# Output-weight sums by accumulating DMAs, and a lighter branch B, in a hybrid attention layer

## The chip, the cores and the metric

One core of one Trainium2 chip runs the whole layer in one launch. The metric is the device time of one execution in microseconds (us), the median of several runs. The engines are TensorE (PE), VectorE (DVE), ScalarE (ACT), GpSimd (POOL) and SyncE (SP), which here only issues DMAs.

## What is computed

One layer on 528 positions (512 and 16 learned meta tokens), width 2048. The stream is normalised and projected once (`u @ w_in`) into the columns of two attention branches, their gates and two merge gates.

- Branch A picks 128 keys for each query by an indexer score and attends to latent keys, 8 heads of 128.
- Branch B takes, for each of 8 heads, `softmax(q1 k1 + bias) - lambda * softmax(q2 k2 + bias)` over chunk-causal keys (64 wide), times the values, and then a root-mean-square norm of every head's output, times a weight:

```python
attn = probs(q1, k1) - lam * probs(q2, k2)
...
o_b = (rms_norm(o_b, subln_w) * (1.0 - lam_init)).reshape(Bsz, T, B_WIDTH)
y_a = (o_a * jax.nn.silu(z_a)) @ w_o_a
y_b = (o_b * jax.nn.silu(z_b)) @ w_o_b
mix = jax.nn.sigmoid(g_a) * y_a + jax.nn.sigmoid(g_b) * y_b
out = mix @ w_out
return h + rms_norm(out, post_w)
```

## The kernel before, in words

The work is laid out in stages, each bound to its matmuls: the first weights and the norm (0 to 78 us), the indexer's projections (to 183), branch B (to 536), branch A (to 775), the gates with a Strassen-like scheme on 2x2 halves (`Pair`, `Run`; to 1221), the two output projections `wo` with the merge (to 1396), and the last product with `w_out`, again in a Strassen-like scheme.

**Weights.** Every weight block is loaded as float32 (`raw`, L144 in the indexer's stage, L179 for a `Unit`, both on SP's queue), squared on ACT with a sum by rows (L117), its maximum taken over the partitions on POOL (`over_rows`, `rows`, L122), turned into a power of two by tiny operations on DVE (`power_of_two`, L129 to L135), and split into a high and a low half-precision part (ACT L161, DVE L162), which PE multiplies (L265 to L267). So PE can't start on a unit before POOL has given its `rows`.

**Branch B.** For head `h` the loop (L845 to L866) projects q, k and v and, between those projections, takes a step of head `h-1`, kept in `pending`: `vprep`, four query blocks `blk(0..3)`, `tr` (PE transposes the probabilities `pr`, L658) and `pv`. Rounds of branch A's top-k (`run_topk`, MAX8 and MATCH_REPLACE8 on DVE) stand between too. `blk` makes two logits, `softmax` for each (DVE adds the bias and takes the maximum, L643; L647 or L649 negates it; ACT takes the exponent, L651), normalises both with the reciprocals of their sums (L724 to L726) and joins them (L727). `kstack` splits the keys of both halves, each copied to both halves of the partitions (ACT `kh` L752 and L753, DVE `kl` L755).

**Sums of output weights.** The last product needs four differences of quarters of `w_out`, for 16 pieces (k, n). `wt_load` (L251) loads four tiles 128x512 on SP's queue, `wt_sums` (L258) takes four differences on DVE (L261) and writes them with four DMAs of ACT's queue to `wout_t1` to `wout_t4`. Heads 1 to 7 of branch B do two pieces each, the `wo` stage the last two. `tc.keep_in_program_order` keeps those loads where they are written.

**GpSimd.** POOL also adds the bias to branch A's scores (L817), takes half of the differences of `t_prep` (L877, L879), multiplies branch B's outputs with their norm (`load_o`, L1048), and clears a corner of the bias tile (L636).

**What sets the order.** The kernel is written for a framework that reorders: a list scheduler gives each engine and queue one fixed order, by its own estimates, and puts in the waits. An instruction that waits holds up all that stands behind it on its engine, DMAs that this engine issues included. Loads stay in a few buffers; at most eight DMAs of a kind (hardware queue, or POOL's) are under way before the ninth waits for the first.

```python
def wt_sums():
    k, n, (b11, b12, b21, b22) = wt["loaded"].pop(0)
    for i, (o, x, y) in ((0, (b11, b12, b11)), (2, (b12, b22, b12)), (1, (b22, b22, b11)), (3, (b21, b21, b22))):
        nc.vector.tensor_sub(o, x, y)
        nc.scalar.dma_start(tscr[i][k, :, 512 * n:512 * n + 512], o)
```

Of the kernel before, what the change touches and what calls it, by code (L numbers as in the profile page):

```python
# [68 lines left out]
def layer_kernel(ctx, tc, xt_d, xn_d, cols_d, w0_d, wi_d, wkv_d, wo_d, wout_d, lam_d, post_d,  # L69
# [11 lines left out]
    msq = nc.dram_tensor("o_sumsq", [NH, 512], F32, kind="Internal").ap()  # L81
    rsq = nc.dram_tensor("o_rstd", [NH, 512], F32, kind="Internal").ap()
# [36 lines left out]
    def over_rows(ssq):  # L119

        r = wpool.tile([P, 16], F32, tag="rows", name="rows", bufs=4)[:, :ssq.shape[1]]
        nc.gpsimd.partition_all_reduce(r, ssq, P, bass_isa.ReduceOp.max)  # L122
        return r

    def power_of_two(r, exps):
# [8 lines left out]
        nc.vector.tensor_scalar(sc[:, 0:1], t, -1.0, SFIELD * EXP1, op0=ALU.mult, op1=ALU.add)  # L134
        nc.vector.tensor_scalar(sc[:, 1:2], t, exps, None, op0=ALU.add)  # L135
# [3 lines left out]
    def exps_with(dst, un, less=0.0):  # L139
        nc.vector.tensor_scalar(dst, un.bitcast(I32), (UFIELD - 127.0 - less) * EXP1, None, op0=ALU.add)  # L140
# [30 lines left out]
    class Unit:  # L171
# [14 lines left out]
        def scale(self):  # L186
            self.s, self.un = power_of_two(self.rows, uexp[:, 1:2] if self.key[0] == "qb" else uexp[:, 0:1])
            self.hi = wpool.tile([P, KT, P], F16, tag="hi", name="hi", bufs=2)
            self.lo = wpool.tile([P, KT, P], F16, tag="lo", name="lo", bufs=2)
# [56 lines left out]
    wt = {"next": 0, "loaded": []}  # L246

    def wt_load(pool, tags):
        k, n = divmod(wt["next"], 2)
        wt["next"] += 1  # L250
        t = []  # L251
        for tag, (ci, di) in zip(tags, ((0, 0), (0, 1), (1, 0), (1, 1))):
            t.append(pool.tile(HB, F32, tag=tag, name="wt"))
            d = nc.sync.dma_start(t[-1], wout_d[ci, di, k, :, 512 * n:512 * n + 512])
            tc.keep_in_program_order(d)
        wt["loaded"].append((k, n, t))

    def wt_sums():  # L258
        k, n, (b11, b12, b21, b22) = wt["loaded"].pop(0)
        for i, (o, x, y) in ((0, (b11, b12, b11)), (2, (b12, b22, b12)), (1, (b22, b22, b11)), (3, (b21, b21, b22))):  # L260
            nc.vector.tensor_sub(o, x, y)  # L261
            nc.scalar.dma_start(tscr[i][k, :, 512 * n:512 * n + 512], o)
# [200 lines left out]
    def u_scale():  # L463
# [4 lines left out]
        s, un = power_of_two(over_rows(gsum), UFIELD * EXP1)  # L468
        nc.vector.tensor_scalar(gs, cols[:, :KT], s, None, op0=ALU.mult)
        exps_with(uexp[:, 0:1], un)  # L470
        exps_with(uexp[:, 1:2], un, 3.0)
# [147 lines left out]

    PH = ap_.tile([P, 11, P], F32R, name="PH")  # L620
# [12 lines left out]
    def bias_tile(h):  # L633
        g = ap_.tile([P, T], F32, tag="G", name="G", bufs=2)
        nc.sync.dma_start(g, bass.AP(tensor=frep, offset=h * P * NF + P - 1, ap=[[NF - 1, P], [1, T]]))
        nc.gpsimd.memset(g[:64, T - 64:T], NEG)  # L636
        return g

    def softmax(srcs, bias, dst, mx, z):
        at = 0  # L640
        for i, x in enumerate(srcs):
            n = x.shape[1]
            nc.vector.tensor_tensor_reduce(dst[:, at:at + n], x, bias[:, at:at + n], 1.0, -3.0e38,  # L643
                                           ALU.add, ALU.max, mx[:, i:i + 1])
            at += n
        if len(srcs) == 2:
            nc.vector.tensor_scalar(mx[:, :1], mx[:, :1], mx[:, 1:2], -1.0, op0=ALU.max, op1=ALU.mult)  # L647
        else:
            nc.vector.tensor_scalar(mx[:, :1], mx[:, :1], -1.0, None, op0=ALU.mult)  # L649
        mx = mx[:, :1]  # L650
        nc.scalar.activation(dst, dst, AF.Exp, bias=mx, accum_out=z)  # L651
# [39 lines left out]
    def b_attend(h, q, kk, vt):  # L691
        q1, q2 = q
# [17 lines left out]
        def blk(b):  # L710
            mx = ap_.tile([P, 8], F32, tag="mx", name="mx", bufs=MXB)
            z = ap_.tile([P, 2], F32, tag="z", name="z", bufs=3)
            n = NKB[b]
            gb = g[:, T - n:T]
            dst = [pr[b], ap_.tile([P, T], F32, tag="p2", name="p2", bufs=4)[:, :n]]
            for m, qm in ((0, q1), (1, q2)):
                qs = qm[:, b * P:(b + 1) * P]
                src = []
                for s in [slice(0, NLB[b])] if b < 3 else [slice(0, TH), slice(TH, T)]:
                    lg = bank1()  # L720
                    mm2(lg[:, :s.stop - s.start], qs, kk[m][0][:, s], kk[m][1][:, s])
                    src.append(lg[:, :n if b < 3 else TH])
                softmax(src, gb, dst[m], mx[:, 2 * m:2 * m + 2], z[:, m:m + 1])
# [21 lines left out]

    def kstack(acc, un):
        out = [[ap_.tile([P, T], F32R, tag="kk", name=n, bufs=6) for n in ("kh", "kl")] for _ in range(2)]
        for t in range(2):
            s = slice(TH * t, TH * t + TH)
            for m, (kh, kl) in enumerate(out):  # L750
                hs, os_ = slice(64 * m, 64 * m + 64), slice(64 - 64 * m, 128 - 64 * m)
                nc.scalar.activation(kh[hs, s], acc[t][hs, :TH], AF.Copy, scale=un[hs])  # L752
                nc.scalar.activation(kh[os_, s], acc[t][hs, :TH], AF.Copy, scale=un[hs])  # L753
                for d in (hs, os_):
                    nc.vector.scalar_tensor_tensor(kl[d, s], acc[t][hs, :TH], un[hs], f32(kh[hs, s]),  # L755
# [488 lines left out]
    for c in range(KT):  # L1244
# [20 lines left out]
        if c in (4, 7):  # L1265
            wt_sums()
# [188 lines left out]
```

## Time and profile before

| | |
|---|---|
| median of 3 runs | 1559.57 us (1557.87 to 1562.82) |
| the profiled execution | 1558.4 us, of which the span of the trace is 1556.6 us |
| PE busy | 1443.3 us, 93% of the span |
| DVE, ACT, POOL busy | 1161.6, 982.9, 150.3 us |
| mean granted clock of PE | 0.971 |
| DMA | 246.7 MB, mean 158 GB/s |

PE is the engine to read against: what the kernel can win is PE's idle time and the time in which PE runs at the lower of its two clocks (1.2 instead of 2.4 GHz, shown as 0.50). The time beside the span (1.8 us) is start and end and stays as it is.

### The profile page before, as it was taken

What the parts mean: (1) busy time and instruction counts of PE and PEld (TensorE: products, weight loads), DVE (VectorE), ACT (ScalarE), POOL (GpSimd) and SP (SyncE); (2) the same over time, 40 slices, a digit from 0 to 9 for tenths busy, and PEclk for the clock granted to TensorE, in tenths of its full rate; (3) what the DMA queues carried; (4) which work ended last, traced back from release to release, by engine and by line L of the source; (5) the groups of instructions that cost most, each with busy time, mean ns of one, the idle gap of its engine ahead of it and who ended that gap; (6) DMA issues with size and microseconds to landing.
All of it is one profiled execution on the core that took longest, in us unless ns stands there. A gap on an engine that the chain in (4) does not pass through costs nothing. (4 is left out here: it accounts for less than half of the span.)

```text
span 1556.6 us, 25582 instructions
## 1 busy us (share of the span) xinstructions
PE 1443.3 (93%) x9474; PEld 1079.9 (69%) x9474; DVE 1161.6 (75%) x2328; ACT 982.9 (63%) x1749; POOL 150.3 (10%) x203
## 2 busy tenths in 40 slices
PE   7899998898988898999998889999999899999997
PEld 7688766766666666556587768888888544458885
DVE  7975888778888786565677777787778566566778
ACT  7364676656566676666676677777778544436555
POOL 3500000000000022212001100000000011000001
PEclk9899999999999999999999989999999999999999
DMA  6482365445545433122544534444445566446774
GB/s 208 147 272 77 123 203 163 151 141 190 196 140 193 136 116 118 53 96 69 186 155 154 162 116 136 137 141 135 135 144 166 186 211 205 147 167 225 240 248 147
DMA packets 98141, 246.70 MB, mean 158 GB/s; under 512 B 11144, under 2 KB 15432, under 8 KB 97888
## 3 DMA queue, kind: packets, MB, share of 16 engines
q1 hardware_dynamic: 81424, 215.44, 43.5%
q10 hardware_dynamic: 16592, 29.64, 5.1%
q8 instruction: 74, 1.21, 0.3%
q14 instruction: 51, 0.42, 0.1%
HBM read 203.01 MB, written 47.39 MB: 161 GB/s over the span
## 5 line engine op out<-in xcount | busy, mean ns | idle before, releaser
L969 PEld LDWEIGHTS <-wh 128*128 128x128 f16 x2464 | 243.5, 99 | 66.7 <-issue 25.0
L117 ACT ACTIVATE junk<-raw 128x1024 bf16<-128x1024 f32 x192 | 202.1, 1053 | 116.7 <-DMA raw<-in_wi_dram 84.9
L265 PE MATMUL acc<-u,hi 128*128 128x264 f16 (+1 forms) x832 | 267.6, 322 | 1.0 <-DVE kal L783 1.0
L266 PE MATMUL acc<-u,hi 128*128 128x264 f16 (+1 forms) x832 | 267.0, 321 | 0.0
L267 PE MATMUL acc<-u,lo 128*128 128x264 f16 (+1 forms) x832 | 267.0, 321 | 0.0
L969 PE MATMUL acc<-tu,wh 128*128 128x256 f16 x1408 | 237.3, 275 | 20.9 <-DVE r L978 16.1
L969 PE MATMUL acc<-tu,wl 128*128 128x256 f16 x704 | 193.5, 275 | 0.0
L969 PE MATMUL acc<-u,wh 128*128 128x256 f16 x1056 | 180.2, 277 | 9.9 <-ACT wh L161 9.9
L161 ACT ACTIVATE hi<-raw,scale 128x1024 f16<-128x1024 f32 x104 | 118.0, 1143 | 108.2 <-PE acc L266 106.2
L162 DVE SCALAR_TENSOR_TENSOR lo<-raw,scale,hi 128x1024 f16<-128x1024 f32 x104 | 132.9, 1283 | 41.9 <-ACT hi L161 41.2
L265 PEld LDWEIGHTS <-hi 128*128 128x128 f16 x1088 | 108.2, 99 | 79.8 <-issue 6.6
L267 PEld LDWEIGHTS <-lo 128*128 128x128 f16 x1088 | 108.0, 99 | 76.8 <-issue 1.9
L162 DVE SCALAR_TENSOR_TENSOR wl<-S,scale,wh 128x1024 f16<-128x1024 f32 x88 | 115.3, 1311 | 59.8 <-ACT wh L161 59.6
L266 PEld LDWEIGHTS <-hi 128*128 128x128 f16 x1088 | 108.1, 99 | 74.3 <-issue 2.1
L969 PE MATMUL acc<-u,wl 128*128 128x256 f16 x528 | 146.3, 277 | 3.5 <-DVE wl L162 3.5
L122 POOL PARTITION_ALL_REDUCE rows<-ssq x90 | 47.8, 531 | 974.9 <-ACT junk L117 880.6
L969 PEld LDWEIGHTS <-wl 128*128 128x128 f16 x1232 | 121.9, 99 | 20.1 <-DVE wl L162 4.8
L161 ACT ACTIVATE wh<-S,scale 128x1024 f16<-128x1024 f32 x88 | 100.2, 1140 | 33.5 <-DVE S L1076 33.5
L267 PE MATMUL acc<-og,lo 128*128 128x512 f16 x256 | 97.0, 379 | 0.0
L265 PE MATMUL acc<-og,hi 128*128 128x512 f16 x256 | 97.0, 379 | 0.0
L266 PE MATMUL acc<-og,hi 128*128 128x512 f16 x256 | 97.0, 379 | 0.0
L162 DVE SCALAR_TENSOR_TENSOR wl<-raw,scale,wh 128x1024 f16<-128x1024 f32 x66 | 85.4, 1294 | 14.1 <-ACT wh L161 14.0
(309 smaller groups left out, 2978.1 us busy)
## 6 DMA issues: line engine op xcount, KB each, us to landing
raw<-in_wi_dram SPq DMA_DIRECT2D x172, 512.0 KB, 4.3
wt<-in_wout_dram SPq DMA_DIRECT2D x64, 256.0 KB, 4.6
wout_t<-wt ACTq DMA_DIRECT2D x64, 256.0 KB, 3.1
raw<-in_wo_dram SPq DMA_DIRECT2D x32, 512.0 KB, 3.9
raw<-wout_t SPq DMA_DIRECT2D x32, 512.0 KB, 3.9
raw<-in_wout_dram SPq DMA_DIRECT2D x24, 512.0 KB, 4.8
sg<-r ACTq DMA_DIRECT2D x32, 256.0 KB, 3.3
sg<-sg SPq DMA_DIRECT2D x32, 256.0 KB, 3.0
```

The lines of the kernel that those rows point to most:

```text
L117: nc.scalar.activation(j, src, AF.Square, accum_out=dst)
L122: nc.gpsimd.partition_all_reduce(r, ssq, P, bass_isa.ReduceOp.max)
L161: nc.scalar.activation(hi, src, AF.Copy, scale=s)
L162: nc.vector.scalar_tensor_tensor(lo, src, s, hi, op0=ALU.mult, op1=ALU.subtract)
L265: nc.tensor.matmul(out, aH, bH, start=start, stop=False)
L266: nc.tensor.matmul(out, aH, bL, start=False, stop=False)
L267: nc.tensor.matmul(out, aL, bH, start=False, stop=stop)
L969: nc.tensor.matmul(acc, a[:, k, :], b, start=first and k == 0 and x == 0, stop=last and x == 2, skip_group_check=True)
```

## The change

Four things change.

1. **Branch B.** The first softmax is left unnormalised: its sum goes into `Z1`, the joined row is `p1 - lambda*z1/z2 * p2`, and the norm of the head's output takes care of the factor, with `eps * z1^2` in its root; `put_sums` writes the sums once. The maximum is taken negated in the same DVE operation, the exponent with scale -1. The low parts of the keys are made once, not for both halves (`kl`, one tile), the copies of the high parts come by two small DMAs on ACT's queue, and ACT writes two more tiles `QZ` of the queries (zeros in the other half).
2. **Powers of two.** Two tiny DVE operations become one.
3. **Output-weight sums.** `wt_chain` replaces `wt_load` and `wt_sums`: two loads on SP, then DMAs of POOL's queue that add another quarter from DRAM into the tile, and puts, now on SP's queue, between them. In all 32 loads, 64 accumulating DMAs and 64 puts instead of 64 loads, 64 subtractions on DVE and 64 puts on ACT's queue. The signs move to `mix_sums` and to one multiplication of `post` by -1. The loads are no longer kept in program order.
4. **GpSimd.** L817, L877, L879, L1048 and the corner of L636 move to DVE.

The diff, cut to its core:

```diff
-        nc.vector.tensor_scalar(sc[:, 0:1], t, -1.0, SFIELD * EXP1, op0=ALU.mult, op1=ALU.add)
-        nc.vector.tensor_scalar(sc[:, 1:2], t, exps, None, op0=ALU.add)
+        nc.vector.scalar_tensor_tensor(sc, sgn, t, ex, op0=ALU.mult, op1=ALU.add)
...
+    def wt_chain(k, n, tags):
+        t = [opool.tile(HB, F32, tag=tag, name="wt") for tag in tags]
+        q = [[wout_d[ci, di, k, :, 512 * n:512 * n + 512] for di in range(2)] for ci in range(2)]
+        def put(i, x):
+            nc.sync.dma_start(tscr[i][k, :, 512 * n:512 * n + 512], x)
+        def add(x, src):
+            nc.gpsimd.dma_start(x, src, accum_op=ALU.add)
+        nc.sync.dma_start(t[0], q[0][0])
+        nc.sync.dma_start(t[1], q[0][1])
+        yield
+        add(t[0], q[0][1])
+        add(t[1], q[1][1])
+        yield
+        put(0, t[0])
+        put(2, t[1])
+        yield
+        add(t[1], q[0][0])
+        yield
+        put(1, t[1])
+        yield
+        add(t[1], q[1][0])
+        yield
+        put(3, t[1])
...
-            nc.vector.tensor_tensor_reduce(dst[:, at:at + n], x, bias[:, at:at + n], 1.0, -3.0e38,
-                                           ALU.add, ALU.max, mx[:, i:i + 1])
+            nc.vector.tensor_tensor_reduce(dst[:, at:at + n], x, bias[:, at:at + n], -1.0,
+                                           mx[:, i - 1:i] if i else 3.0e38, ALU.add, ALU.min, mx[:, i:i + 1])
...
-            nc.vector.reciprocal(z, z)
-            nc.vector.tensor_mul(z, z, pscale)
-            nc.vector.tensor_scalar(dst[0], dst[0], z[:, 0:1], None, op0=ALU.mult)
+            nc.vector.reciprocal(z[:, 1:2], z[:, 0:1])
+            nc.vector.tensor_scalar(z[:, 1:2], z[:, 1:2], zs, nlam, op0=ALU.mult, op1=ALU.mult)
             nc.vector.scalar_tensor_tensor(dst[0], dst[1], z[:, 1:2], dst[0], op0=ALU.mult, op1=ALU.add)
...
+    def qstack(acc, un, h):
+        q = stack64(acc, un, ap_, "q", 4)
+        for m in range(2):
+            hs = slice(64 * m, 64 * m + 64)
+            nc.scalar.activation(QZ[h % 2][m][hs], acc[hs], AF.Copy, scale=un[hs])
+        return list(q) + QZ[h % 2]
...
+            for m in range(2):
+                hs = slice(64 * m, 64 * m + 64)
+                nc.scalar.activation(kh[m][hs, s], acc[t][hs, :TH], AF.Copy, scale=un[hs])
+                nc.vector.scalar_tensor_tensor(kl[hs, s], acc[t][hs, :TH], un[hs], f32(kh[m][hs, s]),
+                                               op0=ALU.mult, op1=ALU.subtract)
+        for m in range(2):
+            hs, os_ = slice(64 * m, 64 * m + 64), slice(64 - 64 * m, 128 - 64 * m)
+            nc.scalar.dma_start(f32(kh[m][os_]), f32(kh[m][hs]))
...
-            nc.gpsimd.tensor_add(gm[:, :n], g[:, T - n:T], SC[b])
+            nc.vector.tensor_add(gm[:, :n], g[:, T - n:T], SC[b])
...
     for h in range(NH):
+        for i in range(2):
+            wt_now.append(wt_chain(h, i, [f"o{6 + 4 * (h % 2) + 2 * i + x}" for x in range(2)]))
...
-            nc.gpsimd.tensor_mul(o, o, r)
+            nc.vector.tensor_mul(o, o, r)
```

**The order that the change makes.** SP's queue at the end of the indexer's stage, before (`raw_1466` is the 11th of twelve weight halves of that stage, `raw_1570` the 12th, the others belong to the first units):

```order
L144 DMA raw_1466<-in_wi_dram 128x1024 [waits DMAHW3_49,DMAHW1_49,DVE_49]
L179 DMA raw_1527<-in_wi_dram 128x1024 [waits DMAHW6_49,DMAHW2_49,DVE_49]
L179 DMA raw_1529<-in_wi_dram 128x1024 [waits DMAHW7_49,DVE_49]
L179 DMA raw_1538<-in_wi_dram 128x1024 [waits DMAHW4_49,DMAHW0_49,DVE_49]
```

The same place after the change (`raw_1467` is the 11th half, `raw_1528` the first unit's; DMASW is the semaphore of a DMA that POOL issued):

```order
L152 DMA raw_1467<-in_wi_dram 128x1024 [waits DMAHW0_49,DVE_49]
L260 DMA wout_t2<-wt_2324 128x512 [waits DMAHW1_49,DMASW4_49]
L265 DMA wt_2856<-in_wout_dram 128x512 [waits DMAHW2_49]
L260 DMA wout_t2<-wt_2328 128x512 [waits DMAHW3_49,DMASW6_49]
L260 DMA wout_t1<-wt_2851 128x512 [waits DMAHW4_49,DMASW5_49]
L260 DMA wout_t3<-wt_2852 128x512 [waits DMAHW5_49,DMASW7_49]
L260 DMA wout_t1<-wt_2855 128x512 [waits DMAHW6_49,DMASW0_49]
L187 DMA raw_1528<-in_wi_dram 128x1024 [waits DMAHW7_49,DVE_49]
```

The scheduler has moved the chains of all sixteen pieces into the indexer's stage and the first units of branch B: a unit's load now stands behind puts, each of which waits until an accumulating DMA has landed.

POOL from the indexer's stage into branch B, before (`rows` of the units; the memsets prepare branch B):

```order
L122 ISA rows<-ssq 128x2 x2
L625 MEMSET PH 128x128
L625 MEMSET PL 128x128
L625 MEMSET MS 80x512
```

and after, where 27 accumulating DMAs stand ahead of these rows:

```order
L128 ISA rows<-ssq 128x2
L263 DMA wt<-in_wout_dram 128x512 x8
L128 ISA rows<-ssq 128x2
L263 DMA wt<-in_wout_dram 128x512 x18
L646 MEMSET PH 128x128
```

Fifty-four of the 64 additions are issued before the third `rows`, the last two just before the eighth.

DVE around the joining of `pr_3338`, the last block of a head of branch B, before (`kl` and `lo` belong to the next head's keys and weights, MAX to the top-k):

```order
L755 SCALAR_TENSOR_TENSOR kl<-acc,scale,kh 64x264 x2
L724 RECIPROCAL z<-z 128x2
L755 SCALAR_TENSOR_TENSOR kl<-acc,scale,kh 64x264
L725 TENSOR_TENSOR z<-z,pscale 128x2
L755 SCALAR_TENSOR_TENSOR kl<-acc,scale,kh 64x264
L726 TENSOR_SCALAR pr_3338<-pr_3338,z 128x528
L162 SCALAR_TENSOR_TENSOR lo<-raw,scale,hi 128x1024
L727 SCALAR_TENSOR_TENSOR pr_3338<-p_3641,z,pr_3338 128x528
```

and after, the same head (`pr_3305`):

```order
L785 SCALAR_TENSOR_TENSOR kl<-acc,scale,kh 64x264
L170 SCALAR_TENSOR_TENSOR lo<-raw,scale,hi 128x1024
L742 RECIPROCAL z<-z 128x1
L785 SCALAR_TENSOR_TENSOR kl<-acc,scale,kh 64x264
L743 TENSOR_SCALAR z<-z,Z_1809,few 128x1
L620 MAX m_3736<-sc_97 128x8
L744 SCALAR_TENSOR_TENSOR pr_3305<-p_3601,z,pr_3305 128x528
```

Between the reciprocal and the joining, one `kl` and the scaling of the row are gone, `lo` has moved ahead of the reciprocal, and a MAX has come in.

## Rows read from the trace of the kernel before

**Rows 1.** The page's busy time of each engine and the DMA share in 40 slices.

```profile
PE 1443.3 (93%) x9474; PEld 1079.9 (69%) x9474; DVE 1161.6 (75%) x2328; ACT 982.9 (63%) x1749; POOL 150.3 (10%) x203
DMA  6482365445545433122544534444445566446774
```

**Rows 2.** Windows by stage: from:to, us, busy by engine (instructions), PEclk, DMA share, GB/s.

```profile
78.00:183.00 105.00, 104.90 (x509) 82.72 (x510) 72.73 (x121) 63.41 (x119) 2.25 (x9) 1.00 0.46 149
245.00:536.00 291.00, 255.09 (x1771) 189.39 (x1769) 242.35 (x674) 178.88 (x347) 15.17 (x27) 0.94 0.52 170
536.00:775.00 239.00, 224.76 (x1263) 143.67 (x1264) 151.64 (x431) 163.53 (x359) 47.79 (x63) 0.98 0.33 104
825.00:935.00 110.00, 92.11 (x767) 77.34 (x765) 82.82 (x101) 75.68 (x122) 11.24 (x12) 0.92 0.45 140
1221.00:1396.00 175.00, 174.77 (x811) 82.38 (x811) 105.04 (x212) 70.33 (x98) 14.65 (x26) 0.99 0.54 173
```

**Rows 3.** Waits of PE: what it waited for, us in total, times, the longest.

```profile
PE acc L658 <- DVE pr L727: 30.9, 8, 6.1
...
PE acc L969 <- ACT wh L161: 9.9, 3, 4.9
PE acc L658 <- ACT pr L827: 6.9, 7, 2.4
```

**Rows 4.** One such stall on PE's timeline, and the windows in and after it.

```profile
342.20 1.09 PE L658 MATMUL acc<-ident,pr 128*128 128x128 f32 x4 [3.48 <-DVE pr L727]
...
342.20:348.00 5.80, 5.80 (x27) 4.66 (x28) 4.39 (x9) 3.61 (x7) 0.00 (x0) 0.50 0.31 90
```

**Rows 5.** DVE's timeline in that stall: start, us, line, operation.

```profile
338.59 0.48 DVE L755 SCALAR_TENSOR_TENSOR kl<-acc,scale,kh 64x264 fp32r<-64x264 f32 x1
...
339.69 0.49 DVE L726 TENSOR_SCALAR pr<-pr,z 128x528 f32<-128x528 f32 x1
340.10 1.28 DVE L162 SCALAR_TENSOR_TENSOR lo<-raw,scale,hi 128x1024 f16<-128x1024 f32 x1
341.29 0.76 DVE L727 SCALAR_TENSOR_TENSOR pr<-p,z,pr 128x528 f32<-128x528 f32 x1
...
343.13 0.58 DVE L600 MAX8 m<-sc 128x8 f32<-128x400 f32 x1
```

**Rows 6.** Groups of instructions by form: count, busy us, mean ns, then idle time before.

```profile
L755 DVE SCALAR_TENSOR_TENSOR kl<-acc,scale,kh 64x264 fp32r<-64x264 f32 x64 | 31.4, 491 | 16.2 <-ACT kh L753 14.8
L649 DVE TENSOR_SCALAR mx<-mx 128x1 f32<-128x1 f32 x72 | 10.1, 143 | 0.3
L261 DVE TENSOR_TENSOR wt<-wt 128x512 f32<-128x512 f32 x64 | 42.6, 685 | 1.9 <-DMA wt<-in_wout_dram 1.6
L817 POOL TENSOR_TENSOR gm<-G,sc 128x528 f32<-128x528 f32 x8 | 12.2, 1521 | 7.4 <-issue 7.4
```

**Rows 7.** POOL's timeline in the gates' stage: start, us, operation, idle before.

```profile
864.71 1.30 POOL L1048 TENSOR_TENSOR o<-o,rb 128x512 f32<-128x512 f32 x1 [4.50 <-DMA rb<-o_rstd]
874.20 0.39 POOL L122 PARTITION_ALL_REDUCE rows<-ssq  x1 [8.19 <-issue]
...
900.01 0.39 POOL L122 PARTITION_ALL_REDUCE rows<-ssq  x1 [9.53 <-issue]
```

**Rows 8.** DVE's timeline at the last of these.

```profile
900.43 0.16 DVE L129 TENSOR_REDUCE exp<-rows 128x1 f32<-128x4 f32 x1 [6.78 <-POOL rows L122]
```

**Rows 9.** DMA issues: queue, count, KB each, median us to landing; the issue's own ns.

```profile
wt<-in_wout_dram SPq DMA_DIRECT2D x64, 256.0 KB, 4.6
wout_t<-wt ACTq DMA_DIRECT2D x64, 256.0 KB, 3.1
...
L254 SPq DMA_DIRECT2D wt<-in_wout_dram x64: 328/426/1384, 208.5 to 1291.3; - x64
```

**Rows 10.** Windows of the stretch into which the chains move (columns as in rows 2).

```profile
92.00:96.00 4.00, 4.00 (x22) 3.37 (x21) 3.90 (x7) 3.46 (x7) 0.00 (x0) 1.00 1.02 401
96.00:104.00 8.00, 8.00 (x42) 6.55 (x41) 7.79 (x14) 6.60 (x14) 0.00 (x0) 1.00 1.05 305
...
70.00:234.00 164.00, 159.69 (x877) 122.13 (x876) 122.63 (x274) 101.29 (x185) 4.42 (x16) 0.99 0.54 174
```

**Rows 11.** POOL's timeline: the eighth `rows` of a unit.

```profile
234.03 0.84 POOL L122 PARTITION_ALL_REDUCE rows<-ssq  x1 [18.54 <-ACT junk L117]
```

More of the change, by code (lines that the diff above doesn't have):

```diff
@@ L99, in layer_kernel @@
     nc.vector.tensor_scalar(gsub, cols[:, 20:21], 1.0 - LAM_INIT, None, op0=ALU.mult)
-    pscale = const.tile([P, 2], F32, name="pscale")
     gs = const.tile([P, KT], F32, name="gs")
-    uexp = const.tile([P, 2], F32, name="uexp")
+    few = const.tile([P, 16], F32, name="few")
+    sgn, ex0 = few[:, 0:2], few[:, 2:4]
+    for i, (x, y) in enumerate(((-1.0, SFIELD), (1.0, UFIELD))):
+        nc.vector.memset(sgn[:, i:i + 1], x)
+        nc.vector.memset(ex0[:, i:i + 1], y * EXP1)
+    uex = {}
+    nlam = few[:, 14:15]
     uH, uL = [None] * KT, [None] * KT
@@ L244, in weights, with wt_step @@
         return hi, lo
[L246 to L262, printed above, removed]
+    def wt_chain(k, n, tags):
[21 more added lines that the diff above has]
+        put(3, t[1])
+    wt_now = []
+    def wt_step():
+        for g in list(wt_now):
+            if next(g, "end") == "end":
+                wt_now.remove(g)
     def mm3(out, aH, aL, bH, bL, start, stop):
@@ L618, in run_topk @@
             f()
+    Z1 = ap_.tile([P, NH * NB], F32, name="Z1")
     PH = ap_.tile([P, 11, P], F32R, name="PH")
@@ L843, in step, with between @@
                 pending.pop(0)()
+    def between():
+        wt_step()
+        run_topk(TK.pop(0))
     for h in range(NH):
+        for i in range(2):
+            wt_now.append(wt_chain(h, i, [f"o{6 + 4 * (h % 2) + 2 * i + x}" for x in range(2)]))
         for acc, un in proj_q("qb", h):
             step(2 if len(pending) == 7 else 1)
-            run_topk(TK.pop(0))
-        q = stack64(acc, un, ap_, "q", 4)
-        for i in range(2 if h else 0):
-            wt_load(opool, [f"o{6 + 4 * ((h + i) % 2) + x}" for x in range(4)])
+            between()
+        q = qstack(acc, un, h)
         for acc, un in proj_kv("kb", h):
             step()
-            run_topk(TK.pop(0))
+            between()
         kk = kstack(acc, un)
@@ L857, in layer_kernel @@
             small_weights(0)
-        for i in range(2 if h else 0):
-            wt_sums()
         for acc, un in proj_kv("vb", h):
             step()
-            run_topk(TK.pop(0))
+            between()
         vt = ap_.tile([P, T], F32, tag="vt", name="vt", bufs=1)
@@ L892, in layer_kernel, with put_sums @@
     run_topk(1000)
+    def put_sums():
+        pt = psum()
+        nc.tensor.transpose(pt[:NH * NB, :P], Z1, ident)
+        zt = ap_.tile([NH * NB, P], F32, name="zt")
+        nc.scalar.copy(zt, pt[:NH * NB, :P])
+        nc.sync.dma_start(zscr.rearrange("h (b p) -> (h b) p", p=P), zt)
     for h in range(NH):
@@ L949, in scale @@
         def scale(self):
[L950 removed]
+            self.s, self.un = power_of_two(self.rows, uex[False])
         def q(self, nm):
@@ L1034, in wide @@
         return zp.tile(HB, F32, tag="r", name=nm, bufs=bufs)
-    rv = zp.tile([P, 32], F32, name="rv")
+    rv, zv = [zp.tile([P, 32], F32, name=n) for n in ("rv", "zv")]
     nc.sync.dma_start(rv, msq.rearrange("h (a b) -> (h a) b", b=32))
-    rstd_cols(rv, rv, P)
+    nc.sync.dma_start(zv, zscr.rearrange("h (a b) -> (h a) b", b=32))
+    nc.vector.tensor_mul(zv, zv, zv)
+    nc.vector.scalar_tensor_tensor(rv, zv, P * EPS, rv, op0=ALU.mult, op1=ALU.add)
+    nc.scalar.activation(rv, rv, AF.Sqrt, scale=1.0 / P)
+    nc.vector.reciprocal(rv, rv)
     nc.sync.dma_start(rsq.rearrange("h (a b) -> (h a) b", b=32), rv)
@@ L1247, in layer_kernel @@
             sgs.append(load_sg(c + 2))
-        if c in (3, 6):
-            wt_load(yp, [f"w{x}" for x in range(4)])
         for ab in range(2):
```

90 lines of the change are left out of this document (42 added, 48 removed).

## The prediction

> **What bounds the kernel now.** First the page: PE is busy for 93% of the span, DVE for 75%, POOL for 10%, and the DMA engines are half busy [rows 1]. So PE is the bound, and only two things can be won: time in which PE stands still, and time in which it runs at its lower clock. The windows by stage say where these lie [rows 2]. In the indexer's stage PE is busy 104.90 of 105 us, and in the `wo` stage 174.77 of 175: nothing to win there, whatever is taken from DVE. In branch B it lacks 35.9 of 291 us and the mean clock is 0.94, which is worth at most 6% of 291, another 17.5 us. In branch A 14.2 of 239 us are missing, in the gates' stage 17.9 of 110 at a clock of 0.92 (8.8 us). These three stages hold some 95 us.
>
> Then the list of PE's waits names what ended last [rows 3]: 30.9 us in 8 waits for the joined row L727 (branch B, once per head), 9.9 us for the weights' high part `wh` (gates), 6.9 us for `pr` L827 (branch A).
>
> One of the eight, closely [rows 4]: PE stands still for 3.48 us, and then runs at 0.50, the lower of the two levels, for 5.8 us, which costs another 2.9. The price of such a stall is thus nearly twice the gap. DVE is what PE waits for, and DVE has no gap there [rows 5]: in front of the joining it does low parts of keys at 0.48, the row's scaling at 0.49 and a 1.28 us split.
>
> In the gates' stage the releaser of the long gaps is POOL, though it is busy for only 11 of 110 us [rows 2]: between a product of branch B's output and the next `rows`, and back, it stands still for 8.19 and 9.53 us with nothing to wait for [rows 7], and DVE waits 6.78 us for such a `rows` [rows 8]. The change of the kind of instruction costs it, not the work.
>
> **The parts.**
>
> *Branch B, the joining.* After the reciprocal there stood two `kl`, the scaling of the row, a tiny product and the split `lo`; now there stand one `kl`, a tiny operation and a MAX8 of 0.58 us. By the durations of rows 5 that is 3.8 us before against 2.2 after, joining included: 1.6 us. Ahead of it another `kl` and two tiny operations on the maximum (0.14 us each [rows 6]) are gone, so 1.6 to 2.5 us per head. Eight stalls of 3.9 us in the mean [rows 3] lose 13 to 20 us; I take 15. The stalls don't vanish, so the low clock after them doesn't either; where they become half as long I count 7 of the 17.5 us. Branch B: **-22**, with 12 (no clock) and 45 (the stalls gone with their clock) as ends.
>
> *The rest of DVE's relief in branch B.* 64 differences of 0.685 us, half of the 31.4 us of `kl`, and 72 negations (10.1 us) go [rows 6]: nearly 70 us of DVE. I cost all of it at nothing beyond the term above, since PE covers DVE elsewhere in this stage (242 of 291 us busy against PE's 255 [rows 2]). On ACT two operations for `QZ` per head come in and four copies `kh` go, and two small DMAs take their place; they stand beside PE as well. If those DMAs were late by 1 us per head, 8 us of the term would be lost.
>
> *Branch A.* The addition to the scores took POOL up to 1.52 us [rows 6]; on DVE a tile of nearly the same size takes 0.685 (the row of L261). 32 additions and 16 differences are at most 32 x 0.7 + 16 x 0.4 = 29 us more for DVE, which has 87 us free of 239 [rows 2]. What goes is POOL's change of kind ahead of the scores and with it most of the 6.9 us: **-5**, ends 0 and -10.
>
> *Gates.* POOL now has only `rows` left until the end; no change of kind remains, so `rows` comes at once after the squares. The three waits for `wh` (9.9 us) go, and with them about half of the 8.8 us of low clock: **-14**. Against it: the eight products with the norm stand on DVE now, in a fixed order, and the tile they need comes by a DMA for which POOL was seen to wait 4.50 us [rows 7]; if DVE has to wait so, it holds up the splits. Ends -3 and -22.
>
> *The chains, the one part that can cost much.* They are 160 transfers of 256 KB, 41.9 MB, moved from branch B into 70 to 234 us, a stretch where PE had no gap to spare. Three bounds:
>
> - In series. A tile's chain is a load, three additions and three puts, and every tile's place serves four pieces in turn. With 4.6 us for a load and 3.1 for a put [rows 9] that is 4 x (4.6 + 9.3 + 3 La) = 55.6 + 12 La. No addition by DMA is in this trace; the nearest row is the load of the same size, 4.6 us, so 111 us of the 164: hidden. It would bind from La = 9 us. From below 3.1 us, the put.
> - By bytes. The stretch moves 174 GB/s x 164 us = 28.5 MB now [rows 10], of which 4.2 MB are sums that the chains replace. 24.3 + 41.9 = 66.2 MB. The fullest windows of the same stretch, with the DMA engines at a share of 1.02 to 1.05, move 401 and 305 GB/s [rows 10]. So 165 to 217 us: the last chain would end at 235 to 287 us. The last additions stand before the eighth `rows`, which came at 234.0 [rows 11]. Delay 1 to 53 us; at the mean rate of 353 GB/s it ends at 258, **+24**.
> - By POOL's issue, a rival below.
>
> A delay of the units' loads or `rows` is PE's own, because PE has no other work there and the stage before is full. I take +24 with ends 0 and 55.
>
> *Small.* One multiplication of `post` on ACT and one transpose for `Z1` lie beside other work: 0 to +2. The one tiny operation less per power of two is off PE's path in the stages that are full.
>
> **Sum**, against the profiled execution's own 1558.4 us: -22 - 5 - 14 + 24 = -17, or **1541 us**. The median of the runs is 1.2 us higher, within what three runs differ. About 0.3%, 4.7 us, is what a measurement of this kernel can tell from no change.
>
> **The rivals.**
>
> 1. *The chains are hidden.* The DMA engines deliver the higher of the two rates, or more, because a chain's transfers fit between the others. Then the delay is 1 us or less: 1558.4 - 41 = **1517**. For it: 401 GB/s was seen. Against: for 4 us only.
> 2. *The DMA engines are full, and the change is slower.* Place: SP's queue and POOL in 70 to 240 us, where a unit's load stands behind puts that wait for additions. At 305 GB/s the delay is 53, and PE, standing still between units, spends some of it at the lower clock as after the stall of rows 4 (four stalls, some 3 us each at most; I take 4 in all): 1558.4 - 41 + 57 = **1574**. It decides from the rate at which delay and gains are equal, 66.2 MB in 164 + 41 us, 323 GB/s. For it: the 8 us window at 305 with a share of 1.05. An addition also has to read and write its target, which no row prices.
> 3. *POOL's issue.* An addition is issued by POOL, in order with `rows`. SP's issue takes 0.43 us, at most 1.4 [rows 9]; 64 of those are 27 to 90 us, hidden. If POOL is held for as long as a short load takes, 3.6 us, 64 make 230 us, and the end is at 300: 1558.4 - 41 + 66 = **1583**. The threshold is 164 / 64 = 2.6 us. The Trainium skill's page "SBUF — State Buffer" (§ A bandwidth-pool intuition that's wrong) speaks against the change just here: a DMA issued by GpSimd needs descriptors which it can't write while certain VectorE operations hold a shared port, and one of about 0.62 us took about 3.1 us beside a VectorE copy. With 3.1 us for each of the 64 the end would be an estimated 268 us and the time about 1551 us. No row of this trace shows it, for there is no DMA of POOL in it. DVE is busy for 69% of the indexer's stage [rows 2], mostly with operations that run one element after another (1.28 us for 1024 a partition [rows 5]), so I give the whole rival little.
> 4. *The gains don't come.* DVE is in order; the MAX8 before the joining and the wait for the norm's tile can keep the stalls at three fourths of their length. Gains of 22 against 24: **1560**, no change.
>
> **How the numbers follow.** The forecast has 0.38 (delays of 10 to 40 us), rival 1 0.22, rival 2 0.22, rival 3 0.08, rival 4 0.10. Faster: nearly all of the forecast and rival 1, 0.58; within 0.3%: rival 4 and a little of the forecast, 0.12; slower: rivals 2 and 3, 0.30. The likeliest case alone reaches from 1526 to 1556. The range of 8 in 10 goes from rival 1 with somewhat more of branch B (-50) at 1508 to rival 2 with a few us more, 1580; above lie rival 3 and the tail of rival 2, below the case that all stalls of branch B vanish and the chains cost nothing.
>
> **What the profile after would show.** Right: PE's list of waits has L658 at about 15 us and no wait above 1 us for `wh` after a late `rows`; POOL has no idle time in the gates' stage that ends with nothing to wait for; DVE's busy time in branch B falls by a fifth or more. The end of the indexer's stage, the first unit's matmul and the first `pr` transposes come some 24 us later than now, with the DMA share near 1 from 75 us on. Wrong in my sense: a start of branch B that isn't late (rival 1), or PE waiting there for 50 us and more (rivals 2 and 3: in the one the DMA share is 1 and an addition lands after 5 us or more, in the other the share is low and POOL's queue stands). If L658 still waits 25 us or more, the term of branch B was wrong; if `wl` or `wh` wait behind a product with `rb`, that of the gates.

## The result, and the profile after

The changed kernel takes **1600.16 us** (median of 4 runs, 1598.25 to 1604.09) against 1558.8 for the kernel before in the same comparison: ratio 1.0263, 95% interval 1.0235 to 1.0292. It is slower by 2.6%, where 1541 us was forecast; 1600 lies above the range, which ended at 1580. The profiled execution took 1604.09 us, the longest of the four; its span is 1602.1.

The page after, the busy time and the DMA share [rows 1]:

```profile
PE 1435.1 (90%) x9475; PEld 1076.2 (67%) x9475; DVE 1103.8 (69%) x2091; ACT 977.2 (61%) x1735; POOL 144.8 (9%) x199
...
DMA  6499999932333323333264544444444544547674
GB/s 208 144 303 271 253 262 263 252 93 83 97 100 88 97 81 87 113 120 99 67 198 157 185 160 141 149 140 132 132 133 145 197 149 155 155 124 260 227 248 155
```

From the third slice to the eighth (80 to 320 us) the DMA engines are full, at some 260 GB/s; in branch B, where the sums used to be, they are a third busy. The windows of the stages (columns as in [rows 2]) show what that did, and what the rest of the change won:

```profile
78.00:310.00 232.00, 148.18 (x752) 112.31 (x750) 98.95 (x209) 87.42 (x158) 61.65 (x82) 0.83 0.98 270
...
302.00:622.00 320.00, 291.45 (x2070) 217.15 (x2071) 221.36 (x607) 206.92 (x407) 9.55 (x24) 0.96 0.34 101
622.00:840.00 218.00, 208.85 (x1197) 132.22 (x1196) 155.47 (x406) 153.08 (x334) 4.43 (x9) 1.00 0.37 114
840.00:1261.00 421.00, 399.07 (x3622) 354.11 (x3621) 338.55 (x409) 322.05 (x495) 13.25 (x26) 1.00 0.47 152
```

The share is 0.98 over 232 us, and PE, which had no gap in the indexer's stage, stands still for 84 us of them, at a mean clock of 0.83. PE's list of waits (what for, us in total, times, the longest) says by what in its first and in its line on the joining [rows 3]:

```profile
PE lg L549 <- ACT relu L570: 39.3, 3, 26.6
PE acc L675 <- DVE pr L744: 17.4, 7, 6.4
```

PE waits for ACT, and ACT, on its own timeline, for a weight:

```profile
165.84 1.06 ACT L123 ACTIVATE junk<-raw 128x1024 bf16<-128x1024 f32 x1 [29.16 <-DMA raw<-in_wi_dram]
```

ACT stood 29 us until a weight's DMA had landed. PE's longest wait ends just behind it, at ACT's `relu`:

```profile
168.45 0.59 PE L549 MATMUL lg<-ikh,q 128*128 128x264 f32 x1 [26.61 <-ACT relu L570]
```

POOL's side (L263 are the additions: ns of an issue, min/median/max; below, the time to landing):

```profile
L263 POOL DMA_DIRECT2D wt<-in_wout_dram x64: 853/862/2252, 78.8 to 309.6; - x64
...
DMA to landing us min/median/max: 3.9/7.6/12.8
```

For the length of each stage I use three marks on PE: the transposes of the values, `vt` (first and last in branch B), the first gate matmul with `tu`, the first of `wo` with `og` (count: ns min/median/max, first to last start). Before:

```profile
L700 PE MATMUL acc<-ident,vt x32: 272/273/474, 215.6 to 551.9; 128*128 128x128 f32 x32
...
L969 PE MATMUL acc<-tu,wh x1408: 269/273/421, 779.0 to 1225.6; 128*128 128x256 f16 x176
L265 PE MATMUL acc<-og,hi x256: 379/379/380, 1215.2 to 1390.3; 128*128 128x512 f16 x128
```

After:

```profile
L716 PE MATMUL acc<-ident,vt x32: 270/273/477, 302.0 to 622.5; 128*128 128x128 f32 x32
...
L1015 PE MATMUL acc<-tu,wh x1408: 269/273/418, 840.0 to 1271.5; 128*128 128x256 f16 x176
L289 PE MATMUL acc<-og,hi x256: 379/379/380, 1261.4 to 1436.2; 128*128 128x512 f16 x128
```

So branch B begins 86.4 us late; then branch B (from the first `vt` to the last) takes 320.5 instead of 336.3 us, branch A 217.5 instead of 227.1, the gates 421.4 instead of 436.2. That is 86.4 - 15.8 - 9.6 - 14.8 = +46.2 us. The two spans differ by 45.5, the two medians by 41.

### The profile page after: what moved, and what is told of

Read it like the earlier page. It is cut to its first block, busy times and chain, and to the rows that moved or that the text cites. A ratio compares the mean times of both kernels' runs of the same rounds, so it can differ in the third digit from the quotient of the medians.

```text
span 1602.1 us, 25286 instructions
## 1 busy us (share of the span) xinstructions
PE 1435.1 (90%) x9475; PEld 1076.2 (67%) x9475; DVE 1103.8 (69%) x2091; ACT 977.2 (61%) x1735; POOL 144.8 (9%) x199
## 3 DMA queue, kind: packets, MB, share of 16 engines
q0 software_dynamic: 9216, 16.78, 6.1%
## 5 line engine op out<-in xcount | busy, mean ns | idle before, releaser
L1015 PE MATMUL acc<-u,wh 128*128 128x256 f16 x1056 | 175.3, 273 | 0.0
L128 POOL PARTITION_ALL_REDUCE rows<-ssq x90 | 43.9, 488 | 1085.8 <-ACT junk L123 1029.3
L1015 PEld LDWEIGHTS <-wl 128*128 128x128 f16 x1232 | 120.8, 98 | 14.4
L158 DVE TENSOR_TENSOR lo<-raw,hi 128x1024 fp32r<-128x1024 f32 x40 | 48.8, 1223 | 73.9 <-ACT hi L156 73.5
```

Source lines behind the costliest of these rows:

```text
L158: nc.vector.tensor_sub(lo, raw, f32(hi))
L1015: nc.tensor.matmul(acc, a[:, k, :], b, start=first and k == 0 and x == 0, stop=last and x == 2, skip_group_check=True)
```

## The experiments

Ratios are to the kernel before on the same chip, with 95% intervals; the experiments used four chips, on which that kernel took 1561.7 to 1565.6 us in the median. "Start" is the first `vt`; B, A and gates are the lengths between the marks, of one profiled execution each.

| run | ratio (interval) | start | B | A | gates |
|---|---|---|---|---|---|
| before | 1 | 215.6 | 336.3 | 227.1 | 436.2 |
| the change | 1.0263 (1.0235 to 1.0292) | 302.0 | 320.5 | 217.5 | 421.4 |
| e1_old_sums | 0.9803 (0.9789 to 0.9818) | 217.8 | 330.6 | 217.4 | 421.7 |
| e2_pinned | 0.9946 (0.9927 to 0.9965) | 223.0 | 343.8 | 219.6 | 426.3 |
| e3_chains_alone | 1.0485 (1.0466 to 1.0503) | 305.0 | 326.9 | 225.5 | 435.9 |
| e4_dve_alone | 0.9842 (0.9810 to 0.9874) | 220.0 | 337.0 | 217.6 | 421.8 |
| e5_branch_b | 0.9973 (0.9949 to 0.9997) | 217.2 | 331.3 | 226.7 | 430.7 |
| e6_plain_dma | 1.0086 (1.0058 to 1.0113) | 271.5 | 318.9 | 217.9 | 426.5 |
| e8_from_head1 | 0.9944 (0.9921 to 0.9968) | 216.6 | 347.2 | 218.9 | 422.1 |
| e9_topk_away | 0.9820 (0.9785 to 0.9855) | 221.5 | 329.1 | 219.6 | 424.9 |
| e10_no_sums | 0.9637 (0.9582 to 0.9693) | 217.2 | 308.6 | 220.0 | 422.3 |
| e11_sums_late | 0.9755 (0.9692 to 0.9818) | 215.6 | 322.9 | 219.8 | 426.2 |
| e12_half_bytes | 1.0050 (1.0018 to 1.0082) | 276.4 | 307.6 | 216.8 | 425.7 |
| e13_dve_late | 0.9829 (0.9776 to 0.9883) | 218.4 | 333.1 | 217.8 | 424.5 |
| e14_few_rows | 0.9785 (0.9751 to 0.9819) | 229.8 | 311.6 | 217.0 | 424.8 |
| e15_pinned_plain | 0.9816 (0.9787 to 0.9845) | 219.1 | 322.5 | 220.2 | 425.2 |
| e16_no_differences | 0.9725 (0.9700 to 0.9751) | 215.6 | 312.4 | 220.1 | 426.2 |

### Which part loses

**e1_old_sums**: the change with `wt_load`, `wt_sums` and their signs as before.

```diff
-            wt_now.append(wt_chain(h, i, [f"o{6 + 4 * (h % 2) + 2 * i + x}" for x in range(2)]))
+        for i in range(2 if h else 0):
+            wt_load(opool, [f"o{6 + 4 * ((h + i) % 2) + x}" for x in range(4)])
...
+        for i in range(2 if h else 0):
+            wt_sums()
```

> The change with the sums of output weights as before (loads kept in order, differences on DVE, puts on ACT's queue), the rest of the change as it is. Theory A (the chains alone cost the time, some 75 us of delay ahead of branch B; the rest wins some 33 us): about 1525 us. Theory B (the rest of the change loses too): 1560 or more.

0.9803, 31 us faster than before. **e3_chains_alone**: the kernel before with the chains and their signs only.

```diff
-            wt_sums()
...
+            wt_now.append(wt_chain(h, i, [f"o{6 + 4 * (h % 2) + 2 * i + x}" for x in range(2)]))
```

> The kernel before with the chains alone (and the signs that belong to them). Theory A: 1559 + 75 = about 1634 us, the DMA share near 1 from 75 to 310 us. If the other parts of the change lose or the delay is shared with them: nearer to 1600.

1.0485, 76 us slower, with the same late start as the change and the DMA share at 0.99 there:

```profile
78.00:310.00 232.00, 152.23 (x756) 115.30 (x754) 101.95 (x220) 87.69 (x159) 59.01 (x79) 0.82 0.99 268
```

The chains alone make the loss; everything else together wins some 31 us. Branch B is 9 us shorter in e3, with the sums gone from it and the end of the chains still in it.

### Why the chains lose

**e6_plain_dma**: POOL's DMAs write instead of adding, so no sums are made.

```diff
-            nc.gpsimd.dma_start(x, src, accum_op=ALU.add)
+            nc.gpsimd.dma_start(x, src)
```

> The change with each accumulating DMA replaced by a plain one of POOL's queue of the same size into the same tile; so the sums of the output weights are not made. If the reading and writing back of the target fills the DMA engines (the trace has 98 us of all sixteen engines for 64 additions, 1.53 us each, against about 0.8 for a plain load): some 45 us less, about 1555 us. If bytes moved, the order in the queues or POOL's issue decide: within 10 us of 1600.

1.0086: 27 us less than the change, between the two answers, and the start is 56 us late instead of 86. The orders of POOL and SP are those of the change. The page's rows on POOL's queue (packets, MB, share of 16 engines) of the change, and then of this run:

```profile
q0 software_dynamic: 9216, 16.78, 6.1%
```

```profile
q0 software_dynamic: 5120, 16.78, 3.0%
```

The same bytes take 6.1% of 1602.1 us, 98 us of all sixteen engines, or 1.53 us for an addition; without adding 3.0% of 1577.5, 0.74 us. Adding costs the DMA engines about twice a plain transfer here.

**e12_half_bytes**: all transfers of the chains at half their columns.

```diff
-        q = [[wout_d[ci, di, k, :, 512 * n:512 * n + 512] for di in range(2)] for ci in range(2)]
+        q = [[wout_d[ci, di, k, :, 512 * n:512 * n + 256] for di in range(2)] for ci in range(2)]
...
-            nc.gpsimd.dma_start(x, src, accum_op=ALU.add)
+            nc.gpsimd.dma_start(x[:, :256], src, accum_op=ALU.add)
```

> The change with every transfer of the chains cut to half its columns (half the bytes, as many DMAs with the same waits, in the same queues; the last product reads quarters of the weights instead of the sums). If the DMA engines' time decides (theory A1): the delay ahead of branch B falls from 86 us by more than half, and the kernel is at 1550 or below. If the number of waits, POOL's issue or the queues' order decide: the delay stays above 60 us and the kernel above 1575.

1.0050, start 61 us late: the delay just meets the second answer, the time (1571 us) neither. The packets stay as many (9216) and the additions still take 3.6% of 1568.9 us, 57 us, so half the bytes are not half the engines' time. The order is not quite the change's either: 36 additions stand ahead of the first `rows` instead of 27, and the last ahead of the fourth instead of the eighth. The share, from 78 us to about the start of branch B, is down only to 0.86:

```profile
78.00:270.00 192.00, 141.85 (x719) 109.85 (x720) 96.61 (x200) 82.16 (x149) 60.61 (x80) 0.85 0.86 218
```

That left it open whether engines' time or the queues' order decides. **e14_few_rows** takes most of the engines' time away and leaves the order: 16 of the 128 rows of each transfer.

```diff
-        q = [[wout_d[ci, di, k, :, 512 * n:512 * n + 512] for di in range(2)] for ci in range(2)]
+        q = [[wout_d[ci, di, k, :16, 512 * n:512 * n + 512] for di in range(2)] for ci in range(2)]
...
-            nc.gpsimd.dma_start(x, src, accum_op=ALU.add)
+            nc.gpsimd.dma_start(x[:16], src, accum_op=ALU.add)
```

> The change with every transfer of the chains cut to 16 of its 128 rows: the same DMAs in the same order with the same waits, one eighth of the bytes and packets (the last product reads quarters of the weights instead of sums). If the DMA engines' time makes the delay: the first head's transposes come within 15 us of the kernel before (86 us late in the change), the DMA share there falls to about 0.55, and the kernel is at about 1510 to 1525, ratio 0.965 to 0.975. If order and latency make it: still 45 us late or more, ratio 0.995 or above.

0.9785, start 14 us late instead of 86, share 0.59:

```profile
110.00:230.00 120.00, 113.29 (x627) 86.80 (x626) 77.60 (x173) 63.98 (x119) 50.16 (x73) 0.97 0.59 150
```

```profile
L263 POOL DMA_DIRECT2D wt<-in_wout_dram x64: 748/1028/1925, 79.0 to 232.1; - x64
...
DMA to landing us min/median/max: 2.3/3.6/8.1
```

The same 64 additions stand in the same places between POOL's `rows`, and each weight behind the same puts; the last is issued at 232 us instead of 310. An addition also lands sooner, in 3.6 us in the median instead of 7.6, so this run alone doesn't part full engines from long landings; the share of 0.98 in the change does, for there the engines had no time left. So the time of the DMA engines makes 72 of the 86 us, the order and the landings that are left at most 14. The chains cost more behind that: in the change they run until 318 us, 16 us into branch B, and with the short transfers that stage takes 311.6 us instead of 320.5.

### The chains elsewhere

**e2_pinned**: every DMA of the chains kept behind what the program has ahead of it on its queue.

```diff
-        nc.sync.dma_start(t[0], q[0][0])
+        tc.keep_in_program_order(nc.sync.dma_start(t[0], q[0][0]))
...
-            nc.gpsimd.dma_start(x, src, accum_op=ALU.add)
+            tc.keep_in_program_order(nc.gpsimd.dma_start(x, src, accum_op=ALU.add))
```

> The change with every DMA of the chains kept behind what the program has ahead of it on its queue, so that the chains spread over the eight heads of branch B. Theory A1 (the chains cost because the scheduler packs 160 transfers into a stretch where the DMA engines then are full): the delay goes, about 1525 us. Theory A2 (accumulating DMAs in order with rows and loads hold up the units wherever they stand): still 1560 or more, with PE waiting for rows in every head.

0.9946: 50 us better than the change (1.0263), but 22 us behind e1. The DMA share is 0.84 in the first head and 0.74 in the rest of branch B, and B is 13 us longer than in e1:

```profile
183.00:245.00 62.00, 54.53 (x372) 38.16 (x371) 34.70 (x111) 32.68 (x58) 14.39 (x20) 0.92 0.84 218
245.00:570.00 325.00, 288.46 (x1986) 216.33 (x1985) 219.60 (x601) 201.08 (x396) 50.74 (x71) 0.93 0.74 191
```

**e8_from_head1**: the same, begun a head later and with four pieces at the last head.

```diff
+        for j in ([h - 1] if 0 < h < NH - 1 else [h - 1, h] if h else []):
+            for i in range(2):
+                wt_now.append(wt_chain(j, i, [f"o{6 + 4 * (j % 2) + 2 * i + x}" for x in range(2)]))
```

> The chains kept in order as in the second run, but begun one head later (two pieces from head 1 on, four at the last), so that nothing of them moves while the first head's weights are loaded. If what the pinned chains still cost (some 22 us over the run with the old sums) lies in the first head, where the DMA engines have a share of 0.84: within 8 us of the run with the old sums, about 1535 to 1540 on the first chip's scale. If each head pays for queues held up by waiting additions: no better than 1556.

0.9944, no better. The start is early again (216.6), but B is no shorter than in e2. PE's waits in e8 (what for, us in total, times, the longest) have the joining:

```profile
PE acc L675 <- DVE pr L744: 39.3, 7, 14.0
```

A single one is 14.0 us long now, at the last head, where four pieces stand together. Ahead of that joining DVE stood still twice, for the keys' high parts (ACT, which makes them, had just waited 7.13 us for a weight) and for a transfer of the bias tile:

```profile
533.13 0.48 DVE L785 SCALAR_TENSOR_TENSOR kl<-acc,scale,kh 64x264 fp32r<-64x264 f32 x1 [6.76 <-ACT kh L784]
...
545.28 0.11 DVE L657 MEMSET G<- 64x64 f32 x1 [4.33 <-DMA G<-bias_rows]
```

From 500 to 545 us the DMA share is 0.93 or more, so the loads come late again. **e15_pinned_plain**: e2 with plain DMAs in place of the additions, so no sums are made.

```diff
-            tc.keep_in_program_order(nc.gpsimd.dma_start(x, src, accum_op=ALU.add))
+            tc.keep_in_program_order(nc.gpsimd.dma_start(x, src))
```

> The pinned chains (1556 us, ratio 0.9946) with plain DMAs of POOL's queue in place of the accumulating ones. If what they cost over the old sums (22 us) is the accumulation's time on the DMA engines: near the run with the old sums, ratio 0.980 to 0.985. If it is the order of waits in SP's and POOL's queues: 0.992 or above.

0.9816; its interval holds e1's 0.9803. The orders of POOL and SP are the same as in e2, so what the pinned chains cost, 20 us, is the accumulation.

### What the rest wins

**e4_dve_alone**: the kernel before with five operations moved.

```diff
-            nc.gpsimd.tensor_mul(o, o, r)
+            nc.vector.tensor_mul(o, o, r)
```

> The kernel before with only the five operations of GpSimd moved to DVE. By the prediction's terms (branch A 5, gates 14): about 19 us faster than before, most of it between 825 and 935 us, POOL without idle time that ends with nothing to wait for there. If DVE has to wait for the tile with the norm, or POOL's change of kind wasn't on PE's path: within 5 us of before.

0.9842, 25 us. In the profiled execution branch A is 9.5 us shorter and the gates 14.4, and branch B begins 4.4 late. POOL in the gates' stage, where each `rows` now waits for ACT's squares and nothing else [rows 7]:

```profile
857.63 0.60 POOL L122 PARTITION_ALL_REDUCE rows<-ssq  x1 [20.55 <-ACT junk L117]
877.76 0.54 POOL L122 PARTITION_ALL_REDUCE rows<-ssq  x1 [19.53 <-ACT junk L117]
898.04 0.37 POOL L122 PARTITION_ALL_REDUCE rows<-ssq  x1 [19.75 <-ACT junk L117]
```

**e5_branch_b**: e1 with those five back on GpSimd.

```diff
-            nc.vector.tensor_mul(o, o, r)
+            nc.gpsimd.tensor_mul(o, o, r)
```

> The kernel before with only the edits of branch B and the shorter power of two; sums of output weights and GpSimd's operations as before. By the prediction's term: about 22 us faster. If the joining still waits for the exponents as long as in the run with the old sums (24.6 us in 7 waits): about 12 us faster, which with the other part adds up to the 31 us that run won.

0.9973, 4 us (0.5 to 8). The joining is waited for 26.0 us in 7 waits instead of 30.9 in 8 [rows 3]. Where the rest stayed is on DVE's timeline, at the joining two heads behind that of [rows 5]. Before:

```profile
431.95 0.08 DVE L643 DVE_READ_ACCUMULATOR2_ANT mx<- 128x1 f32 x1
431.95 0.71 DVE L600 MAX8 m<-sc 128x8 f32<-128x528 f32 x1
...
437.43 0.76 DVE L727 SCALAR_TENSOR_TENSOR pr<-p,z,pr 128x528 f32<-128x528 f32 x1
```

The same head in e1:

```profile
431.33 0.71 DVE L604 MAX8 m<-sc 128x8 f32<-128x528 f32 x1
...
433.80 0.08 DVE L649 DVE_READ_ACCUMULATOR2_ANT mx<- 128x1 f32 x1
433.80 0.48 DVE L769 SCALAR_TENSOR_TENSOR kl<-acc,scale,kh 64x264 fp32r<-64x264 f32 x1
434.20 1.26 DVE L170 SCALAR_TENSOR_TENSOR lo<-raw,scale,hi 128x1024 f16<-128x1024 f32 x1
435.40 0.15 DVE L726 RECIPROCAL z<-z 128x1 f32<-128x1 f32 x1
435.47 0.68 DVE L604 MAX8 m<-sc 128x8 f32<-128x528 f32 x1
436.08 0.25 DVE L727 TENSOR_SCALAR z<-z,Z,few 128x1 f32<-128x1 f32 x1
436.36 0.50 DVE L769 SCALAR_TENSOR_TENSOR kl<-acc,scale,kh 64x264 fp32r<-64x264 f32 x1
436.89 0.77 DVE L728 SCALAR_TENSOR_TENSOR pr<-p,z,pr 128x528 f32<-128x528 f32 x1
```

From the last maximum (the accumulator read) to the end of the joining 3.8 us go by instead of 6.2, still filled with other work: a split of 1.26 us, a MAX8, two `kl`. But a step of the top-k that stood behind the last maximum (MAX8, MATCH_REPLACE8) now stands between the maxima, and the last of them comes later. Counted from the head's first logit matmul (426.91 and 427.50 us), the joining ends after 10.2 us instead of 11.3, and PE's wait at this head falls only from 3.90 to 3.45 us. Most of what the edits freed, the order has given to others.

**e9_topk_away**: e1 with the top-k rounds moved away from the last block.

```diff
-    TK = [4, 3, 3, 3, 3, 3] + [2, 1, 2, 1, 2, 1] * 6 + [1, 1, 1, 0, 0, 0]
+    TK = [4, 3, 3, 3, 3, 3] + [3, 3, 3, 0, 0, 0] * 6 + [1, 1, 1, 0, 0, 0]
```

> The run with the old sums, with the top-k rounds of heads 1 to 6 moved to the projections of q and the first half of k, away from the last block of the softmax. If the top-k operations between the maxima are what keeps the joining late: the waits of the transposes for it fall from 24.6 to about 15 us and the time by 10 us or more. If the chain maximum, exponent, split and joining is as long without them: within 3 us of that run.

0.9820, as e1: the waits are 22.8 us in 7. At the same joining a second split `lo` now stands instead:

```profile
435.89 2.46 DVE L170 SCALAR_TENSOR_TENSOR lo<-raw,scale,hi 128x1024 f16<-128x1024 f32 x2
```

**e10_no_sums**: e1 without any sums.

```diff
-            nc.vector.tensor_sub(o, x, y)
-            nc.scalar.dma_start(tscr[i][k, :, 512 * n:512 * n + 512], o)
+            pass
```

> The run with the old sums without any sums of output weights: no loads, differences or puts for them; the last product reads quarters of the weights in their place, as many bytes. It bounds what the sums cost where they stand now, in branch B. Heads of branch B were 42.5 to 44 us apart in the change, where no chain moves any more, and 44 to 49 in the run with the old sums: about 22 us faster than that run, ratio to the kernel before about 0.966. If PE hides the sums fully, as the prediction held: within 4 us of that run (0.980).

0.9637: the sums cost 26 us (17 to 35) where they stood, not nothing; branch B falls from 330.6 to 308.6. **e16_no_differences**: e1 without the differences, with loads and puts.

```diff
-            nc.vector.tensor_sub(o, x, y)
             nc.scalar.dma_start(tscr[i][k, :, 512 * n:512 * n + 512], o)
```

> The run with the old sums (ratio 0.980) without the 64 differences on DVE, all loads and puts kept (so quarters of the weights are written where sums belong). If DVE is what the sums cost in branch B: near the run without sums, ratio about 0.965. If the transfers are it: about 0.980.

0.9725, 12 us (8 to 16) better than e1, B 312.4. So some half of the 26 us is the 64 differences on DVE (42.6 us of its time [rows 6]), the rest by subtraction the transfers; in branch B alone 18 of 22 us are DVE's. The stages behind it are 7 us longer in e16 than in e1, for which no run shows a reason. PE's wait for the joining drops to 16.2 us in 7 waits, from e1's 24.6:

```profile
PE acc L658 <- DVE pr L727: 16.2, 7, 5.1
```

**e11_sums_late** and **e13_dve_late**: four of the pieces moved from heads 4 to 7 to the stage of `wo`, in e1 and in e4.

```diff
+    PIECES = [0, 2, 2, 2, 1, 1, 1, 1]
...
-        if c in (3, 6):
+        if c in (1, 3, 5, 7, 9, 11):
```

> The run with the old sums, with six of the sixteen pieces done in the stage of wo instead of two, and one instead of two in each of heads 4 to 7. If a piece costs 1.5 to 2 us in branch B and nothing in the stage of wo, where PE never waits: some 7 us faster than that run, ratio about 0.976. If the stage of wo then waits for DVE or loads: no better than 0.980.

> The kernel before with GpSimd's five operations on DVE, and with six pieces in the stage of wo as in the run before last, without any edit of branch B. If the edits of branch B are worth 4 to 6 us and late sums 7: about 1562 - 25 - 7, ratio about 0.980. If late sums win nothing: 0.984.

0.9755 and 0.9829. In e11 branch B is 7.7 us shorter than in e1, but the gates' stage of that execution is 4.5 longer, and the interval (0.9692 to 0.9818) holds e1's ratio: the gain over e1 isn't shown. In e13 there is none over e4 within the interval. e11, at 1527.5 us, is the fastest run that leaves nothing out, by its ratio too; e1 and e11 both beat both kernels.

## Why the prediction was wrong, by its own steps

**The chains, the term that failed.** The place and the mechanism were those of rival 2: a unit's load behind full DMA engines, PE standing still at a lower clock. What failed is the step "by bytes", and with it the +24. It took 353 GB/s, the mean of two short windows, one of them 4 us long, as the rate of a full stretch. Measured were 270 GB/s over 232 us. With that, 66.2 MB take 245 us, from 70 to 315, a delay of 81 us. The eighth `rows` came 89 us later than before [rows 11], the start of branch B 86:

```profile
323.37 0.35 POOL L128 PARTITION_ALL_REDUCE rows<-ssq  x1 [12.88 <-ACT junk L123]
```

Two things are in the gap between 353 and 270. The mean of short windows was too high even for plain transfers: e6, with as many bytes and no adding, was at 312 GB/s in its full stretch,

```profile
78.00:280.00 202.00, 149.77 (x760) 113.86 (x759) 102.08 (x212) 88.35 (x158) 40.59 (x82) 0.87 0.92 312
```

where the forecast's own arithmetic gives 212 us, an end at 282 and a delay of 48 (56 measured). The rest, from 312 to 270 and some 30 us of the delay, is the addition. Rival 2 named it ("An addition also has to read and write its target, which no row prices") and then left it without a price. So the end of the range was set by 305 GB/s, the lower of two rates of plain transfers, where an unpriced operation called for a lower one.

**The series** (55.6 + 12 La) with the landing times after, 4.8 for a load, 5.9 for a put and 7.6 for an addition: 4 x (4.8 + 17.7 + 22.8) = 181 us. That is more than the stretch's 164 us, so at these landings, which are those of full engines, it would no longer have been hidden. But the chains took from 72 to 318 us, so it isn't what bound them. In e14, with the same order and short landings, the eighth `rows` is 9 us late.

**POOL's issue** (rival 3): 0.86 us in the median, against the threshold of 2.6. It fell. No run shows the rule of the Trainium skill that I weighed there ("SBUF — State Buffer", § A bandwidth-pool intuition that's wrong) at work: in e15 POOL's plain DMAs of 256 KB land in 3.4 us in the median, SP's loads of that size in 5.0.

**Branch B, -22.** The change's stage is 15.8 us shorter, and both signs named for the term came: PE waits 17.4 us for the joining, and DVE's busy time in the stage (third of the busy times) falls by a fifth. But it did not come by the step that was given, so the size is in part luck. Before and after, then e5 and e16:

```profile
215.60:551.90 336.30, 297.44 (x2073) 223.50 (x2074) 280.25 (x799) 212.59 (x417) 16.72 (x30) 0.94 0.51 167
302.00:622.50 320.50, 291.95 (x2075) 217.65 (x2076) 221.83 (x611) 207.42 (x408) 9.55 (x24) 0.96 0.34 101
217.20:548.50 331.30, 296.33 (x2076) 220.92 (x2075) 255.86 (x658) 207.71 (x405) 10.58 (x30) 0.95 0.54 175
215.60:528.00 312.40, 288.30 (x2075) 215.87 (x2074) 222.08 (x609) 208.51 (x407) 8.85 (x22) 0.98 0.57 186
```

The edits of the joining, forecast at -15 with the clock's 7, are worth 4 us (e5), and with them alone PE still waits 26.0 us; the order filled the freed time. The sums' leaving is worth 9 (e3) with the end of the chains in the stage, and some 19 without it (e14 against e1). "I cost all of it at nothing" was wrong: PE covers DVE in the stage's sum, but in the chain before each joining DVE has no gap [rows 5], and without the differences alone the stage is 18 us shorter (e16 against e1). Why 34 us less of DVE's time are worth 18 there, and the 24 us less of the edits 5, no run shows; e9, which moved DVE's work and took none away, won nothing.

**Branch A, -5, and gates, -14.** 9.5 and 14.4 in e4, 9.6 and 14.8 in the change. Right for the gates, and PE's list has no wait for `wh` any more, as forecast; low by half for A. The gates won their 14 us although DVE does the products with the norm now.

**The sum.** Measured 86 - 16 - 10 - 15; forecast 24 - 22 - 5 - 14. The gains were right in total (40 and 41), which is luck: branch B's came for another reason and fell short by about as much as branch A and the gates were above; the forecast loss was little over a quarter of the measured one.

## What to carry to other kernels

Before moving transfers into a full stage, count the DMA engines' time of the stretch, not the issue slots, and take for an operation without a row a rate below the lowest seen. Where a scheduler may reorder, read where it has put the transfers, and keep in program order those that must not run ahead: that alone gave back 50 of the 72 us between the change and e1. And time freed on an engine in front of the critical step is worth something only if nothing else that is ready takes its place.

## What was not expected

An addition by DMA took the sixteen DMA engines 1.53 us for 256 KB, a plain DMA of the same queue 0.74, with 9216 packets against 5120 for the same 16.78 MB. And 64 differences on DVE that seemed hidden beside PE cost 12 us (8 to 16) of the whole kernel, nearly as much as all of GpSimd's changes of kind in the gates' stage.
